# Reciprocal roots of the norms on GpSimd, and a longer page allowance, in a two-layer decoder step

## The chip, the cores and the metric

The kernel runs on one core of a Trainium2 chip. A core has five engines with instruction queues of their own: TensorE (PE, with PEld for its weight loads), VectorE (DVE), ScalarE (ACT), GpSimd (POOL) and SyncE (SP), and 16 DMA engines between the main memory and the on-chip memories. Each engine works through its queue in order, and waits on semaphores for what others make. The metric is the device time of one execution in microseconds (us), less is better; the median over runs counts.

## The reference

One inference step of two layers on 512 prompt tokens and 8 samples of 8 new tokens each (576 columns in all), float32, model width 1024. Layer 0 is a gated DeltaNet (a recurrence over chunks, 8 groups of two heads), layer 1 is differential attention over keys and values made by a shared projection, for the samples also over 1024 cached tokens each, in 8 pages of 128 tokens. What matters here are the norms:

```python
def rms_norm(x, gain):
    xf = x.astype(F32)
    y = xf * lax.rsqrt(jnp.mean(xf * xf, axis=-1, keepdims=True) + NORM_EPS)
    return (y * gain.astype(F32)).astype(x.dtype)

def l2_normalize(x):
    return x * lax.rsqrt(jnp.sum(x * x, axis=-1, keepdims=True) + NORM_EPS)
...
    q = jnp.repeat(l2_normalize(q.reshape(b, L, GDN_QK_HEADS, GDN_DK)) * GDN_DK ** -0.5, rep, axis=2)
    k = jnp.repeat(l2_normalize(k.reshape(b, L, GDN_QK_HEADS, GDN_DK)), rep, axis=2)
...
    o = rms_norm(o, out_gain) * jax.nn.silu(z.astype(F32)).reshape(b, L, GDN_V_HEADS, GDN_DV)
...
    k = partial_rotary(rms_norm(k.reshape(b, L, DIFF_HEADS, 2, DIFF_DH).astype(F32), k_gain), cos, sin)
...
    q = partial_rotary(rms_norm(q.reshape(b, L, DIFF_HEADS, 2, DIFF_DH).astype(F32), q_gain), cos, sin)
...
    o = rms_norm(o, sub_gain) * (1.0 - lam_init)
```

There is also a norm of the residual stream ahead of each layer and of the shared keys and values.

## The kernel before

Activations lie transposed, 128 of the model's dimensions on the partitions and the 576 tokens in two halves of 288 columns. A weight comes in sets of 1024 x 128 numbers (512 KB). For accuracy, weights and activations are each split into a rounded part and a rest (hi and lo); a product is three matrix products: hi by hi, hi by lo, lo by hi. In layer 0 the weights' rest is made by an accumulating DMA that POOL issues (L927, L937), in layer 1 by two POOL subtractions of 512 columns for each set (split_w, L2018).

The work runs in three stages: an opening (class Opening: the residual's norm and the first modulation), the first layer (class Weave) and the second (class Second). In each the order of the instructions on PE, ACT, DVE and POOL is laid out ahead of time by a planner in the kernel's own code: pieces of work are Python generators that yield an engine letter, a price in us and conditions, the planner keeps a clock for each engine, takes at each step the piece that can start first (a lower rank wins a tie), and fixes the resulting order of each engine. "E" and "L" stand for PE, "A" for ACT, "D" and "S" for DVE, "P" and "Q" for POOL. "S" and "P" also share a modelled port, so the plan lets no "S" step overlap a "P" step; "D" and "Q" do not take the port. A step behind another engine's starts HOP = 0.2 us after it, on PE PAD = 0.5 us. A room is one of a named set of buffers: a step that asks for one waits until it is left. A DMA is modelled as 2.3 us of latency, its price on a shared channel, and LATE = 0.6 us from its end until its data counts as landed.

The change touches these places:

- rsqrt (L160) and rsqrt_steps (L177): y = 1/sqrt(x) for a [128, n] tile, as an integer first guess (L167, L181), half of x (L169, L183) and three Newton steps of three instructions (L171 to L173, L186 to L188), 11 DVE instructions. rsqrt issues them as one step, rsqrt_steps as four, so that other DVE work can come between.
- Opening.sums: the root of the first norm, for 5 columns.
- Group.prep and Group.post: for each of the 8 groups of the first layer the keys' root (5 columns) and the output norm's (9 columns).
- second_norm: the residual's root in the second layer, once for each half.
- Tile2.rows: the 16 tiles of queries and keys, each evacuated by ACT, transposed, squared, summed over 64 (L2272), scaled (L2275), rooted (10 columns), multiplied by the root (L2278), and transposed back on PE. Tile2.rotary does the rotary part in four POOL instructions (L2304 to L2307) ahead of L2278.
- Prompt2.finish: the output norm of each of 8 attention heads over the prompt.
- samples_end: the output norm of the samples. The root is spread to all partitions by scaling the identity (L2638), a product with ones, and a copy to the on-chip memory (L2644).
- transfers (L333): what the planner takes as landed, and when. Cached pages ("kpage", "vpage") are loaded by Pages.loads into five rooms: POOL copies the page's number (L2471), SP reads it and issues the DMA (L2476). Sample2.keys (tile px) and Sample2.values (tile po) use two pages at a time on PE.

Of the other lines that the prediction names, L2224 evacuates a tile of the z projection of layer 1, and L1416 copies a part of the first layer's recurrence.

Of the kernel before, what the change touches and what calls it, by code (L numbers as in the profile page):

```python
# [10 lines left out]
F32 = mybir.dt.float32  # L11
F32R = mybir.dt.float32r
BF16 = mybir.dt.bfloat16
I32 = mybir.dt.int32
# [4 lines left out]
D = 1024  # L19
# [140 lines left out]
def rsqrt(K, pool, x, n, parts=128, tag="rs"):  # L160

    nc = K.nc
    y = pool.tile([128, n], F32, name=tag + "y", tag=tag + "y")
    t = pool.tile([128, n], F32, name=tag + "t", tag=tag + "t")
    xh = pool.tile([128, n], F32, name=tag + "h", tag=tag + "h")
    s = slice(0, parts)
    nc.vector.tensor_scalar(out=y[s].bitcast(I32), in0=x.bitcast(I32), scalar1=-0.5,  # L167
                            scalar2=float(0x5F3759DF), op0=ALU.mult, op1=ALU.add)
    nc.vector.tensor_scalar(out=xh[s], in0=x, scalar1=-0.5, scalar2=None, op0=ALU.mult)  # L169
    for _ in range(3):  # L170
        nc.vector.tensor_mul(out=t[s], in0=y[s], in1=y[s])  # L171
        nc.vector.tensor_mul(out=t[s], in0=t[s], in1=xh[s])
        nc.vector.scalar_tensor_tensor(out=y[s], in0=t[s], scalar=1.5, in1=y[s], op0=ALU.add, op1=ALU.mult)  # L173
    return y


def rsqrt_steps(K, pool, x, n, tag, us):  # L177

    nc = K.nc
    y, t, xh = (pool.tile([128, n], F32, name=tag + c, tag=tag + c) for c in "yth")  # L180
    nc.vector.tensor_scalar(out=y[:].bitcast(I32), in0=x.bitcast(I32), scalar1=-0.5,  # L181
                            scalar2=float(0x5F3759DF), op0=ALU.mult, op1=ALU.add)
    nc.vector.tensor_scalar(out=xh[:], in0=x, scalar1=-0.5, scalar2=None, op0=ALU.mult)  # L183
    for _ in range(3):
        yield "S", us
        nc.vector.tensor_mul(out=t[:], in0=y[:], in1=y[:])  # L186
        nc.vector.tensor_mul(out=t[:], in0=t[:], in1=xh[:])
        nc.vector.scalar_tensor_tensor(out=y[:], in0=t[:], scalar=1.5, in1=y[:], op0=ALU.add, op1=ALU.mult)  # L188
    return y
# [64 lines left out]
class Weave:  # L254
# [76 lines left out]
    def transfers(self, until):  # L331

        while True:  # L333
            act = [q for q in self.queues.values() if q]
            rate = SHARED if len(act) > 1 else 1.0
            lands = self.clock + min(q[0][0] for q in act) / rate if act else math.inf
            comes = self.coming[0][0] if self.coming else math.inf
            t = max(self.clock, min(lands, comes))
            if t > until or t == math.inf:
                return  # L340
            for q in act:
                q[0][0] -= (t - self.clock) * rate
            self.clock = t
            if comes <= lands:
                _, _, q, us, name = self.coming.pop(0)
                self.queues[q].append([us, name])
            else:
                for q in act:
                    if q[0][0] < 1e-9:
                        self.done[q.pop(0)[1]] = t + LATE, None  # L350
                return
# [95 lines left out]
class Opening(Weave):  # L447
# [95 lines left out]
    def sums(self):  # L543
# [16 lines left out]
        r = yield from rsqrt_steps(K, K.small, ms[:], nt, "rn", 0.6)  # L560
# [343 lines left out]
SB = 3  # L904
HELD = 4
# [132 lines left out]
class Group:  # L1038
# [196 lines left out]
    def prep(self):  # L1235
# [40 lines left out]
        yield "S", 0.6  # L1276
        ksum = A.sm.tile([128, 5], F32, name="ksum")
        nc.vector.tensor_scalar_add(out=ksum[:], in0=ssk[:], scalar1=4 * EPS)
        rk = yield from rsqrt_steps(K, A.sm, ksum[:], 5, "rs", 0.53)
# [205 lines left out]
    def post(self):  # L1485
# [4 lines left out]
        yield "S", 0.8, ("O", g), ("gdn", g), ("ssq", g), ("sq", g)  # L1490
# [5 lines left out]
        self.rs = yield from rsqrt_steps(K, A.sm, x[:], 9, "ro", 0.6)  # L1496
# [587 lines left out]
def second_norm(W, K, half):  # L2084
# [12 lines left out]
    yield "S", 0.3  # L2097
    r = yield from rsqrt_steps(K, P.ss, ms[:], 3, "rn", 0.6)
# [107 lines left out]
class Tile2:  # L2206
# [41 lines left out]
    def rows(self):  # L2248
# [25 lines left out]
        yield "S", 0.5  # L2274
        nc.vector.tensor_scalar(out=ss[:], in0=ss[:], scalar1=1.0 / 64, scalar2=EPS, op0=ALU.mult, op1=ALU.add)  # L2275
        r = yield from rsqrt_steps(K, P.tk, ss[:], 10, "rq", 0.6)
# [330 lines left out]
def samples_end(W, K):  # L2607
# [12 lines left out]
    yield "A", 0.65, Room("pg"), Room("pg")  # L2620
    r0, r1 = W.took
    ta, tb = (K.pg.tile([128, 8, 128], F32, name="pg")[:].rearrange("p a b -> p (a b)") for _ in range(2))
    sq, d, rt = ta[:, 0:512], ta[:, 512:1024], tb[:, 0:512]
# [10 lines left out]
    yield "S", 2.0  # L2634
    r = rsqrt(K, K.small, ms[:, 0:4], 4, tag="rn")
    yield "S", 1.15
    for c in range(4):
        nc.vector.tensor_scalar(out=d[:, 128 * c:128 * c + 128], in0=K.ident, scalar1=r[:, c:c + 1], scalar2=None, op0=ALU.mult)  # L2638
# [10 lines left out]
    W.leave(r0, r1)  # L2649
# [19 lines left out]
class Prompt2:  # L2669
# [81 lines left out]
    def finish(self, h):  # L2751
# [17 lines left out]
        W.leave(lr)  # L2769
        yield "D", 0.7  # L2770
# [272 lines left out]
def setup(K, ctx, ins):  # L3043
# [21 lines left out]
    K.asel = con[:, 128:e - s]  # L3065
    ones = K.per.tile([128, 128], F32, name="ones")
# [136 lines left out]
```

## Time and profile before

| | us |
|---|---|
| runs shown: median of 3 (lowest, highest) | 1199.89 (1198.29, 1205.4) |
| the profiled execution | 1203.46 |
| its span, from the first to the last instruction | 1201.7 |
| cached pages, 64 of keys and 64 of values, issue to landing (median) | 5.4 and 5.2 |
| bytes moved by DMA | 241.06 MB |

The profile gives each instruction's start and duration, its engine, line and tiles. A wait is idle time of an engine ahead of an instruction, put down to what ended last before it. Lines of the timeline read: start, duration, engine, line, operation, tile written and tiles read, shape, count where several are merged, and in brackets the idle time ahead of it with what ended it. Stages of the execution: the opening up to about 40 us, the first layer to about 660, the residual, q and k projections to 880, pages, prompt heads, v and z projections to about 1147, and the output projection.

### The profile page before, as it was taken

The numbers are of one execution on the slowest core, as the hardware profiler recorded it, in microseconds if no ns is written. First come the engines' busy times: TensorE is split into PE (matmuls) and PEld (weight loads), VectorE is DVE, ScalarE is ACT, GpSimd is POOL, SyncE is SP. The second block draws the span as 40 slices with busy tenths as digits, with TensorE's granted clock in tenths as the row PEclk, the third lists the DMA queues.
The fourth block names the chain that finished last, engine by engine and source line by source line (L and its number), as shares of the span: only waits on it lengthen the run. The fifth ranks groups of instructions, "written<-read, shape, count | busy, mean of one in ns | idle before, by whom it ended". The sixth has DMA issues, their size and how long they took to land.

```text
span 1201.7 us, 33311 instructions
## 1 busy us (share of the span) xinstructions
PE 1147.5 (95%) x12819; PEld 1050.2 (87%) x12819; DVE 766.7 (64%) x2223; ACT 688.0 (57%) x1894; POOL 373.8 (31%) x720
## 2 busy tenths in 40 slices
PE   8999999999999999899989999999999999998998
PEld 6899899998989998899988989998997777777998
DVE  5667876767877876668635467487644555555542
ACT  4766768677776867576545243865435545543430
POOL 2432322241322323232122340656524223121241
PEclk8999999999999999999999999999999999999999
DMA  9786667676666566566958985322948998993243
GB/s 363 211 216 161 156 158 165 178 168 185 175 175 174 135 173 153 179 176 172 255 164 232 337 283 181 106 66 79 346 154 310 326 334 304 346 329 100 58 125 116
DMA packets 87935, 241.06 MB, mean 201 GB/s; under 512 B 14482, under 2 KB 28690, under 8 KB 87778
## 3 DMA queue, kind: packets, MB, share of 16 engines
q1 hardware_dynamic: 71650, 180.22, 43.4%
q0 software_dynamic: 16128, 58.73, 22.2%
q8 instruction: 101, 1.65, 0.6%
q14 instruction: 56, 0.46, 0.1%
HBM read 213.07 MB, written 25.84 MB: 199 GB/s over the span
## 4 chain that ended last, share of the span: by engine, by line
PE 61%; DMA 14%; ACT 8%; issue 7%; DVE 6%; POOL 2%; SPq 1%; POOLq 0%; DVEq 0%; ACTq 0%
PE pp L292 16%; PE pp L1922 10%; PE pc L292 6%; DMA whi<-wall 5%; PE px L1922 5%; PE pq L1922 5%; PE pt L292 3%; PE sc L1922 3%; PE pt L1922 2%; DMA pg<-cv 2%; PE pt L1927 2%; PE po L1922 2%; PE pa L292 2%; PE pv L1922 2%; DMA pg<-ck 2%
## 5 line engine op out<-in xcount | busy, mean ns | idle before, releaser
L2018 POOL TENSOR_TENSOR wlo<-wraw,whi 128x512 fp32r<-128x512 f32 x94 | 122.8, 1327 | 179.0 <-ACT whi L2013 169.4
L292 PE MATMUL pp<-hlo,whi 128*128 128x288 f32 x592 | 172.3, 311 | 0.0
L292 PE MATMUL pp<-hhi,whi 128*128 128x288 f32 x592 | 163.1, 296 | 0.0
L1922 PE MATMUL pp<-hhi,whi 128*128 128x288 f32 x432 | 132.5, 307 | 3.0 <-DVE x L1821 2.3
L1922 PE MATMUL pp<-hlo,whi 128*128 128x288 f32 x432 | 127.6, 296 | 2.0 <-DVE hlo L1847 1.6
L1922 PE MATMUL pp<-hhi,wlo 128*128 128x288 f32 x432 | 125.9, 296 | 0.9 <-POOL wlo L2018 0.6
L292 PE MATMUL pp<-hhi,wraw 128*128 128x288 f32 x576 | 124.8, 301 | 0.0
L292 PEld LDWEIGHTS pp<-hlo,whi 128*128 128x128 f32 x592 | 112.3, 190 | 1.9 <-issue 1.2
L292 PEld LDWEIGHTS pp<-hhi,whi 128*128 128x128 f32 x592 | 112.5, 190 | 0.6
L292 PE MATMUL pp<-hhi,wlo 128*128 128x288 f32 x592 | 104.1, 303 | 0.1
L292 PEld LDWEIGHTS pp<-hhi,wraw 128*128 128x128 f32 x576 | 94.6, 190 | 0.5
L1922 PEld LDWEIGHTS pp<-hhi,whi 128*128 128x128 f32 x432 | 81.4, 188 | 6.6 <-issue 5.3
L1128 DVE SCALAR_TENSOR_TENSOR y<-u,vec,y 128x600 f32<-128x600 f32 x96 | 82.9, 865 | 5.6 <-ACT y L1125 5.1
L292 PEld LDWEIGHTS pp<-hhi,wlo 128*128 128x128 f32 x592 | 84.7, 188 | 2.0 <-issue 1.2
L292 PE MATMUL pp<-hlo,wraw 128*128 128x288 f32 x288 | 84.3, 315 | 0.0
L1922 PEld LDWEIGHTS pp<-hlo,whi 128*128 128x128 f32 x432 | 81.5, 189 | 2.7 <-DVE hlo L1847 2.1
L1922 PEld LDWEIGHTS pp<-hhi,wlo 128*128 128x128 f32 x432 | 80.7, 188 | 1.3 <-POOL wlo L2018 0.8
L937 POOL DMA_DIRECT2D wlo<-wall x38 | 33.7, 887 | 125.8 <-ACT wlo L932 84.9
L2471 POOL COPY pg<-ptt 1x1 int32<-1x1 int32 x128 | 25.8, 206 | 142.3 <-PE px L1922 78.4
L2013 ACT CAST whi<-wraw 128x1024 fp32r<-128x1024 f32 x47 | 49.0, 1046 | 33.8 <-DMA wraw<-wall 9.5
L1922 PE MATMUL pq<-hhi,whi 128*128 128x288 f32 x192 | 61.8, 322 | 3.1 <-DVE x L2224 2.9
L1922 PE MATMUL pq<-hhi,wlo 128*128 128x288 f32 x192 | 57.1, 297 | 0.0
(512 smaller groups left out, 3150.8 us busy)
## 6 DMA issues: line engine op xcount, KB each, us to landing
pg<-ck SPq DMA_DIRECT2D x64, 512.0 KB, 5.4
pg<-cv SPq DMA_DIRECT2D x64, 512.0 KB, 5.2
wraw<-wall SPq DMA_DIRECT2D x49, 512.0 KB, 4.4
whi<-wall POOLq DMA_DIRECT2D x38, 512.0 KB, 6.3
wlo<-wall POOLq DMA_DIRECT2D x38, 512.0 KB, 6.0
wraw<-wall POOLq DMA_DIRECT2D x36, 512.0 KB, 5.9
araw<-ada SPq DMA_DIRECT2D x24, 512.0 KB, 5.2
araw<-ada SPq DMA_DIRECT2D x8, 1024.0 KB, 14.6
```

Source lines behind the costliest of these rows:

```text
L292: return self.K.nc.tensor.matmul(**kw)
L937: K.nc.gpsimd.dma_start(out=lo[:], in_=src, accum_op=ALU.add)
L1128: nc.vector.scalar_tensor_tensor(out=y[:, :YW], in0=u[:, j:j + YW], scalar=cw[j], in1=y[:, :YW], op0=ALU.mult, op1=ALU.add)
L1922: return self.K.nc.tensor.matmul(**kw)
L1927: return self.K.nc.tensor.transpose(**kw)
L2013: nc.scalar.copy(out=hi[:], in_=raw[:])
L2018: nc.gpsimd.tensor_sub(out=lo[:, q:q + 4], in0=raw[:, q:q + 4], in1=hi[:, q:q + 4].bitcast(F32))
L2471: nc.gpsimd.tensor_copy(out=e, in_=P.ptt[0:1, i:i + 1])
```

## The change

The reciprocal root becomes one instruction on POOL, x to the power of -0.5, with a constant tile as the exponent, at all the places above: the 11 DVE instructions go, and the step is planned as "Q" at POW = 1.2 us. The planner counts a cached page as landed SPARE = 1.4 us after its modelled end instead of 0.6. At the samples' end the root is spread to all partitions by four products that read it as their broadcast weights, whose result the last multiplication reads where it lies, so the scalings of the identity, the copy and one of two page rooms go. In the prompt heads two small DVE instructions become one, and a room is left ahead of the root. Some prices of neighbouring "S" steps are lowered to what is left in them.

```diff
-def rsqrt(K, pool, x, n, parts=128, tag="rs"):
...
-    nc.vector.tensor_scalar(out=y[s].bitcast(I32), in0=x.bitcast(I32), scalar1=-0.5,
-                            scalar2=float(0x5F3759DF), op0=ALU.mult, op1=ALU.add)
-    nc.vector.tensor_scalar(out=xh[s], in0=x, scalar1=-0.5, scalar2=None, op0=ALU.mult)
-    for _ in range(3):
-        nc.vector.tensor_mul(out=t[s], in0=y[s], in1=y[s])
-        nc.vector.tensor_mul(out=t[s], in0=t[s], in1=xh[s])
-        nc.vector.scalar_tensor_tensor(out=y[s], in0=t[s], scalar=1.5, in1=y[s], op0=ALU.add, op1=ALU.mult)
-    return y
-
-
-def rsqrt_steps(K, pool, x, n, tag, us):
...
+def root(K, pool, x, n, tag):
+
     y = pool.tile([128, n], F32, name=tag + "y", tag=tag + "y")
...
+    K.nc.gpsimd.tensor_tensor(out=y[:], in0=x, in1=K.power.to_broadcast([128, n]), op=ALU.pow)
     return y
...
-                        self.done[q.pop(0)[1]] = t + LATE, None
+                        name = q.pop(0)[1]
+                        self.done[name] = t + (SPARE if "page" in str(name[0]) else LATE), None
...
+SPARE = 1.4
+POW = 1.2
...
# Opening.sums
-        r = yield from rsqrt_steps(K, K.small, ms[:], nt, "rn", 0.6)
+        yield "Q", POW
+        r = root(K, K.small, ms[:], nt, "rn")
...
# Group.prep
-        yield "S", 0.6
+        yield "S", 0.2
...
-        rk = yield from rsqrt_steps(K, A.sm, ksum[:], 5, "rs", 0.53)
+        yield "Q", POW
+        rk = root(K, A.sm, ksum[:], 5, "rs")
...
# Group.post
-        self.rs = yield from rsqrt_steps(K, A.sm, x[:], 9, "ro", 0.6)
+        yield "Q", POW
+        self.rs = root(K, A.sm, x[:], 9, "ro")
...
# Tile2.rows
-        yield "S", 0.5
+        yield "S", 0.2
         nc.vector.tensor_scalar(out=ss[:], in0=ss[:], scalar1=1.0 / 64, scalar2=EPS, op0=ALU.mult, op1=ALU.add)
-        r = yield from rsqrt_steps(K, P.tk, ss[:], 10, "rq", 0.6)
+        yield "Q", POW
+        r = root(K, P.tk, ss[:], 10, "rq")
...
# samples_end
-    yield "A", 0.65, Room("pg"), Room("pg")
...
+    yield "A", 0.65, Room("pg")
...
-    yield "S", 2.0
-    r = rsqrt(K, K.small, ms[:, 0:4], 4, tag="rn")
-    yield "S", 1.15
-    for c in range(4):
-        nc.vector.tensor_scalar(out=d[:, 128 * c:128 * c + 128], in0=K.ident, scalar1=r[:, c:c + 1], scalar2=None, op0=ALU.mult)
+    yield "Q", POW
+    r = root(K, K.small, ms[:, 0:4], 4, "rn")
...
-    K.mm(out=ps[:], lhsT=K.ones, rhs=d, start=True, stop=True)
-    yield "A", act(512)
-    nc.scalar.copy(out=rt, in_=ps[:])
-    W.leave(xr)
-    yield "S", 0.75
-    nc.vector.scalar_tensor_tensor(out=o, in0=rt.rearrange("p (h t) -> p h t", t=64), scalar=K.sg2[:, 0:1], in1=o,
+    for c in range(4):
+        K.mm(out=ps[:, 128 * c:128 * c + 128], lhsT=r[:, c:c + 1].to_broadcast([128, 128]), rhs=K.ident, start=(c == 0),
+             stop=(c == 3))
+    yield "D", 0.75
+    nc.vector.scalar_tensor_tensor(out=o, in0=ps[:].rearrange("p (h t) -> p h t", t=64), scalar=K.sg2[:, 0:1], in1=o,
                                    op0=ALU.mult, op1=ALU.mult)
...
# Prompt2.finish
-        yield "S", 2.7
+        yield "S", 0.4
...
-        nc.vector.tensor_mul(out=x[:], in0=ls[:, :, 0], in1=ls[:, :, 0])
-        nc.vector.tensor_scalar(out=x[:], in0=x[:], scalar1=EPS, scalar2=None, op0=ALU.mult)
+        nc.vector.scalar_tensor_tensor(out=x[:], in0=ls[:, :, 0], scalar=EPS, in1=ls[:, :, 0], op0=ALU.mult, op1=ALU.mult)
...
-        r = rsqrt(K, P.ss, x[:], 4, tag="ra")
         W.leave(lr)
+        yield "Q", POW
+        r = root(K, P.ss, x[:], 4, "ra")
...
# setup
+    power = K.per.tile([128, 1], F32, name="power")
+    nc.gpsimd.memset(power[:], -0.5)
+    K.power = power[:]
```

The output norm of Group.post and the first norm in second_norm are changed in the same way; the price of the "S" step ahead of the root falls from 0.8 to 0.4 in the first, and the step of 0.3 goes in the second.

More of the change, by code (lines that the diff above doesn't have):

```diff
@@ L157 @@
     pass
-def rsqrt(K, pool, x, n, parts=128, tag="rs"):
-    nc = K.nc
+def root(K, pool, x, n, tag):
     y = pool.tile([128, n], F32, name=tag + "y", tag=tag + "y")
[L164 to L167, printed above, removed]
-                            scalar2=float(0x5F3759DF), op0=ALU.mult, op1=ALU.add)
-    nc.vector.tensor_scalar(out=xh[s], in0=x, scalar1=-0.5, scalar2=None, op0=ALU.mult)
-    for _ in range(3):
-        nc.vector.tensor_mul(out=t[s], in0=y[s], in1=y[s])
-        nc.vector.tensor_mul(out=t[s], in0=t[s], in1=xh[s])
-        nc.vector.scalar_tensor_tensor(out=y[s], in0=t[s], scalar=1.5, in1=y[s], op0=ALU.add, op1=ALU.mult)
-    return y
-def rsqrt_steps(K, pool, x, n, tag, us):
[L179 to L188, printed above, removed]
+    K.nc.gpsimd.tensor_tensor(out=y[:], in0=x, in1=K.power.to_broadcast([128, n]), op=ALU.pow)
     return y
@@ L1489, in post @@
         last = g == G - 1
-        yield "S", 0.8, ("O", g), ("gdn", g), ("ssq", g), ("sq", g)
+        yield "S", 0.4, ("O", g), ("gdn", g), ("ssq", g), ("sq", g)
         x = A.sm.tile([128, 9], F32, name="ox")
@@ L2096, in second_norm @@
     nc.vector.tensor_scalar(out=ms[:], in0=ps[:, HT:HT + 3], scalar1=1.0 / D, scalar2=EPS, op0=ALU.mult, op1=ALU.add)
-    yield "S", 0.3
-    r = yield from rsqrt_steps(K, P.ss, ms[:], 3, "rn", 0.6)
+    yield "Q", POW
+    r = root(K, P.ss, ms[:], 3, "rn")
     yield "E", None
@@ L2619, in samples_end @@
     W.leave(xr)
-    yield "A", 0.65, Room("pg"), Room("pg")
-    r0, r1 = W.took
-    ta, tb = (K.pg.tile([128, 8, 128], F32, name="pg")[:].rearrange("p a b -> p (a b)") for _ in range(2))
-    sq, d, rt = ta[:, 0:512], ta[:, 512:1024], tb[:, 0:512]
+    yield "A", 0.65, Room("pg")
+    r0, = W.took
+    sq = K.pg.tile([128, 8, 128], F32, name="pg")[:].rearrange("p a b -> p (a b)")[:, 0:512]
     nc.scalar.activation(out=sq.rearrange("p (h t) -> p h t", t=64), in_=o, func=AF.Square)
@@ L2641, in samples_end @@
     ps = K.px.tile([128, 512], F32, name="px")
-    K.mm(out=ps[:], lhsT=K.ones, rhs=d, start=True, stop=True)
-    yield "A", act(512)
-    nc.scalar.copy(out=rt, in_=ps[:])
-    W.leave(xr)
-    yield "S", 0.75
-    nc.vector.scalar_tensor_tensor(out=o, in0=rt.rearrange("p (h t) -> p h t", t=64), scalar=K.sg2[:, 0:1], in1=o,
+    for c in range(4):
[3 more added lines that the diff above has]
+    nc.vector.scalar_tensor_tensor(out=o, in0=ps[:].rearrange("p (h t) -> p h t", t=64), scalar=K.sg2[:, 0:1], in1=o,
                                    op0=ALU.mult, op1=ALU.mult)
-    W.leave(r0, r1)
+    W.leave(xr, r0)
     yield from gated2(W, K, slice(0, 8), slice(SEQ, NT), 512, [("z", h, 1) for h in range(8)], ("gs",))
@@ L2762, in finish @@
         W.leave(pvr)
[L2763 removed]
+        yield "S", 0.4
         x = P.ss.tile([128, 4], F32, name="oxx")
[L2765 to L2766 removed]
+        nc.vector.scalar_tensor_tensor(out=x[:], in0=ls[:, :, 0], scalar=EPS, in1=ls[:, :, 0], op0=ALU.mult, op1=ALU.mult)
         nc.vector.scalar_tensor_tensor(out=x[:], in0=ms[:], scalar=1.0 / 128, in1=x[:], op0=ALU.mult, op1=ALU.add)
[L2768 removed]
         W.leave(lr)
+        yield "Q", POW
+        r = root(K, P.ss, x[:], 4, "ra")
         yield "D", 0.7
```

## Prediction

> **What bounds the kernel now.** I read the page first (busy shares), then the busy times by stage, then the waits of PE, and last the timeline around each wait of PE that a root stands behind.
>
> ```profile
> span 1201.7 us, 33311 instructions
> PE 1147.5 (95%) x12819; PEld 1050.2 (87%) x12819; DVE 766.7 (64%) x2223; ACT 688.0 (57%) x1894; POOL 373.8 (31%) x720
> ```
>
> PE is the bound: it is idle for 1201.7 - 1147.5 = 54.2 us. The change takes no matrix work away (below), so what it can win lies in these 54 us. By stage (columns: stretch, length, then busy time and count of PE, PEld, DVE, ACT, POOL, granted clock, DMA share, GB/s):
>
> ```profile
> 0.00:640.00 640.00, 615.52 (x6908) 569.89 (x6909) 448.48 (x1336) 429.12 (x1280) 185.27 (x388) 0.99 0.69 186
> 640.00:760.00 120.00, 114.45 (x1146) 109.44 (x1145) 73.65 (x182) 47.40 (x99) 38.17 (x37) 1.00 0.74 248
> 760.00:880.00 120.00, 113.01 (x1061) 109.62 (x1060) 86.43 (x259) 71.48 (x136) 68.89 (x116) 1.00 0.45 150
> 880.00:1100.00 220.00, 211.89 (x3042) 172.06 (x3041) 110.61 (x335) 111.50 (x319) 52.28 (x157) 1.00 0.84 295
> 1100.00:1202.00 102.00, 92.61 (x674) 89.16 (x672) 47.50 (x114) 28.49 (x61) 29.19 (x22) 0.97 0.31 94
> ```
>
> Idle of PE: 24.5 us in the first layer (0 to 640), 5.6, 7.0 in the stage of the q and k rows (760 to 880), 8.1 in the stage of the cache pages, 9.4 at the end. The waits of PE say for what (total us, times, longest):
>
> ```profile
> PE pc L292 <- ACT wv L1416: 4.7, 10, 1.3
> PE pt L1927 <- DVE qkt L2278: 4.5, 2, 2.7
> PE po L1922 <- DMA pg<-cv: 4.0, 7, 1.2
> PE pq L1922 <- DVE x L2224: 2.9, 3, 2.3
> PE pt L1927 <- DVE qss L2275: 1.8, 1, 1.8
> PE px L1922 <- DMA pg<-ck: 1.6, 3, 0.7
> PE pp L1922 <- POOL wlo L2018: 0.6, 1, 0.6
> ```
>
> The largest group is the first layer's chain on ACT; no root stands in it. The second, fourth and fifth are roots, as the timeline shows, and the third and sixth are the pages.
>
> **The change, part by part.** It has 44 places: 1 in the opening, 8 key norms and 8 output norms in the first layer, 2 residual norms, 16 q and k rows, 8 prompt heads and the samples' end in the second. Each drops 11 DVE instructions (484 in all) and gains one on POOL.
>
> *DVE freed.* The three lines of one Newton step, 48 times each in the 16 q and k rows:
>
> ```profile
> L187 DVE TENSOR_TENSOR rqt<-rqt,rqh 128x10 f32<-128x10 f32 x48 | 13.7, 285 | 1.7
> L188 DVE SCALAR_TENSOR_TENSOR rqy<-rqt,rqy 128x10 f32<-128x10 f32 x48 | 11.8, 246 | 1.6
> L186 DVE TENSOR_TENSOR rqt<-rqy 128x10 f32<-128x10 f32 x48 | 11.4, 239 | 0.7
> ```
>
> Undisturbed such an instruction takes 0.17 us (timeline below), in the rows 0.24 to 0.29 on average. The rows' nine steps are 13.7 + 11.8 + 11.4 = 36.9 us; 484 at 0.17 to 0.29 give 82 to 140, I take 100 us, out of 766.7. DVE is not the bound, so this counts only where PE waits on it.
>
> *Where PE waits for a root: the rows.* Why they are slower than 0.17 us:
>
> ```profile
> 808.89 0.22 DVE L2275 TENSOR_SCALAR qss<-qss 128x10 f32<-128x10 f32 x1
> 809.96 0.36 POOL L2307 TENSOR_TENSOR qkt<-rc,rsn 128x80 f32<-128x80 f32 x1
> 810.78 0.17 DVE L187 TENSOR_TENSOR rqt<-rqt,rqh 128x10 f32<-128x10 f32 x1
> 811.34 2.51 POOL L2018 TENSOR_TENSOR wlo<-wraw,whi 128x512 fp32r<-128x512 f32 x2 [1.02 <-ACT whi L2013]
> 811.40 1.25 DVE L187 TENSOR_TENSOR rqt<-rqt,rqh 128x10 f32<-128x10 f32 x1
> 812.69 1.19 DVE L188 SCALAR_TENSOR_TENSOR rqy<-rqt,rqy 128x10 f32<-128x10 f32 x1
> 813.98 1.03 DVE L2278 TENSOR_TENSOR qkt<-qkt,rqy 128x640 f32<-128x640 f32 x1
> 815.15 0.74 PE L1927 MATMUL pt<-con_ident,qkt 128*128 128x128 f32 x5 [2.71 <-DVE qkt L2278]
> ```
>
> The same DVE instruction takes 0.17 us alone and 1.25 when POOL's weight split begins just before it: it ends when POOL's first of two ends (811.34 + 1.26), the next when the second ends. Two such hits end in 2.71 us of idle PE. The other two waits in this stage:
>
> ```profile
> 775.19 0.74 PE L1927 MATMUL pt<-con_ident,qkt 128*128 128x128 f32 x5 [1.77 <-DVE qss L2275]
> 801.92 0.74 PE L1927 MATMUL pt<-con_ident,qkt 128*128 128x128 f32 x5 [1.74 <-DVE qkt L2278]
> ```
>
> Together 2.71 + 1.77 + 1.74 = 6.22 us. On POOL the root cannot collide with POOL's own split. In the first case its input is there at 809.11 and POOL has ended the rotary at 810.32; a power of 1.2 us ends at 811.5, and the multiplication starts then instead of at 813.98: 2.5 us sooner, 0.2 of the 2.71 stay. The multiplication itself still reads two tiles and can still be hit; I leave 0.8 us for that in the three, so -5.4.
>
> The Trainium skill (GPSIMD Engine Reference, 8. Key points) says that GpSimd shares its SBUF interfaces with VectorE, with contention for instructions that have two SBUF inputs; the rows above agree, 0.17 against 1.25 us. By that rule each power would also hold DVE off while it runs, which the rows of before cannot show.
>
> *The samples' end.*
>
> ```profile
> 1103.93 0.78 DVE L167 TENSOR_SCALAR rny<-nms 128x4 int32<-128x4 int32 x1
> 1106.32 0.16 DVE L173 SCALAR_TENSOR_TENSOR rny<-rnt,rny 128x4 f32<-128x4 f32 x1
> 1106.86 0.44 DVE L2224 SCALAR_TENSOR_TENSOR x<-scr,pq 128x288 f32<-128x288 f32 x1
> 1107.36 0.40 PE L1922 MATMUL pq<-hhi,whi 128*128 128x288 f32 x1 [2.26 <-DVE x L2224]
> ```
>
> The root holds DVE from 1103.93 to 1106.48 in one piece, the evacuation L2224 stands behind it, and PE waits 2.26 us for that bank. With the root on POOL this goes: -2.1 (0.2 kept for a later neighbour). The four scalings by the identity and the copy (L2638, L2644) go as well; one 512-column product becomes four of 128, the same columns with three more weight loads, which overlap other products. Nothing for either.
>
> *The other places.* Opening: the root's first and last instruction, the first product that reads it, and the stretch around it:
>
> ```profile
> 13.72 0.17 DVE L181 TENSOR_SCALAR rny<-nms 128x5 int32<-128x5 int32 x1
> 15.53 0.17 DVE L188 SCALAR_TENSOR_TENSOR rny<-rnt,rny 128x5 f32<-128x5 f32 x1
> 17.91 1.33 PE L292 MATMUL pa<-con_ident,rny 128*128 128x128 f32 x6
> 16.00:36.00 20.00, 18.91 (x196) 0.93 1.04 405
> ```
>
> An undisturbed root takes 15.70 - 13.72 = 1.98 us, and PE reads it 2.2 us after its end. DMA is full (share 1.04, the ada loads) from 16 to 36 us, so a sooner root is hidden; if that cover were gone, it would be worth at most 1.98 - 1.2 = 0.8 us. First layer, residual norms and prompt heads: none is named in a wait of PE, 0, with -4 to +3 kept for the range, since 17 x 2 us of DVE goes there.
>
> *The page allowance.* A page counts as landed 1.4 instead of 0.6 us after its modelled end, so its products are placed 0.8 us later in PE's fixed order. The waits for pages are 4.0 + 1.6 = 5.6 us in 10 pieces of at most 1.2; 0.8 later, little of each would be left. But a page read later frees its room later, the next load is issued later, and DMA is 0.84 busy there. I take half: -2.5; bounds -5 and +6 (below).
>
> *POOL's new work.* 44 powers. No row of before has one. Near rows:
>
> ```profile
> L2304 POOL TENSOR_TENSOR rc<-qkt,cosq x8: 519/533/979, 767.0 to 820.0; 128x160 f32<-128x160 f32 x8
> L2306 POOL TENSOR_TENSOR qkt<-rc,rsn x16: 351/354/389, 768.1 to 875.5; 128x80 f32<-128x80 f32 x16
> L2305 POOL TENSOR_TENSOR rsn<-qkt,sinq x8: 522/611/1106, 767.4 to 820.5; 128x160 f32<-128x160 f32 x8
> L2471 POOL COPY pg<-ptt x128: 173/174/1583, 672.8 to 1083.8; 1x1 int32<-1x1 int32 x128
> L2018 POOL TENSOR_TENSOR wlo<-wraw,whi 128x512 fp32r<-128x512 f32 x94 | 122.8, 1327 | 179.0 <-ACT whi L2013 169.4
> ```
>
> Least 0.17 us (one element); the longest row is 1.33, but a power is more work per element than a subtraction, so rows give no ceiling, and I keep 4 us as the far end, three times the longest row. I take 1.2, the plan's own price, because its other POOL prices agree with rows: 1.29 for the split (row 1.33), 1.85 for the four rotary instructions (0.53 + 0.61 + 0.35 + 0.36). 44 x 1.2 = 53 us lie beside PE: POOL is busy 31%, and 68.89 + 16 x 1.2 = 88 of 120 us in the fullest stage. What is queued behind them in order: weight splits, page copies and the first layer's weight loads. PE waited only 0.6 us for splits all told, so I add +1.5 for such delays.
>
> Sum: -5.4 - 2.1 - 2.5 + 1.5 = -8.5 us. The profiled execution took 1203.46 us (span 1201.7), 3.6 above the median of 1199.89; it becomes 1195.0, and the median 1191.4.
>
> **The rivals.**
> *Given back.* All instructions get new places from the planner, and waits that were hidden come forward. For it: only 13% of PE's idle time is the rows'. Then -1 to -2, 1198.5.
> *More than the waits.* The planner also reckons with about 100 us less DVE and may pack the 24.5 us of the first layer and the 5.6 after it better. If a third of these 30 goes, -10 on top: 1182.
> *The power is long (slower).* Place: the rows' stage, where POOL has 120 - 68.89 = 51 us free; 16 powers fill it at 3.2 us each. An undisturbed root on DVE takes 1.98 us, so from 2.0 us on each undisturbed row is later than now, and at 4 us POOL needs 68.9 + 64 = 133 us of 120, PE +13: 1199.9 + 13 = 1213. Holding DVE off for 16 x 4 us would add to it. Against it: the agreement of the other prices.
> *The allowance slows the pages.* Five rooms serve 128 pages; 0.8 us more per room and turn is 128/5 x 0.8 = 20 us on the pages' stretch if the rooms bind, of which products of the z projection cover most; PE would lose some 6: 1205. Against it: at DMA share 0.84 the transfers, not the rooms, set most of the pace.
>
> **How the numbers follow.** About 1% (12 us) is what a measurement of this kernel tells from no change. Forecast 1191.4 (own range 1186 to 1197): 0.42. Given back 0.22, more 0.20, long power 0.09, slow pages 0.07. Faster than 1187.9: 0.18 from "more" and 0.10 from the low part of the forecast, 0.28. Slower than 1211.9: 0.07 from the long power, 0.05 from slow pages and unlucky placement, 0.12. Within: 0.60. The range takes in most of "more" and "given back" and slow pages: 1180 to 1207.
>
> **What would show it.** Right: DVE near 665 us busy and 484 fewer instructions; POOL +44 instructions and about +53 us; no wait of PE on L2278 above 1 us between 760 and 820; no wait on L2224 above 1 us near the samples' end; waits for pages under 3 us in total. Wrong: a power over 2.0 us; POOL over 100 of 120 us in the rows' stage; PE's idle time still 54 us or more, under new names; or PE busy longer than 1147 us, which nothing here accounts for.

## The result, and the profile after

| | before | after |
|---|---|---|
| median, us (lowest, highest) | 1199.32 (1198.29, 1205.4) | 1185.38 (1184.48, 1191.14) |
| ratio, with its 95% interval | | 0.9866 [0.9834, 0.9899] |
| the profiled execution, us | 1203.46 | 1185.3 |
| its span, us | 1201.7 | 1183.3 |

By the two medians the kernel became 13.9 us faster; the ratio puts the gain at 1.3%. The two profiles differ by 18.4 us, because the one of before comes from an execution 4 us above its median; what follows from a pair of profiles is to be read with that in mind. The page of after, span and busy times:

```profile
span 1183.3 us, 32811 instructions
PE 1145.0 (97%) x12827; PEld 1048.3 (89%) x12827; DVE 685.8 (58%) x1727; ACT 689.8 (58%) x1893; POOL 453.5 (38%) x765
```

PE does the same work (1145.0 against 1147.5 us) and is idle for 38.3 instead of 54.2 us. DVE lost 496 instructions and 80.9 us (484 of the roots, the four scalings at the samples' end, one in each of 8 prompt heads), POOL gained 45 and 79.7 us. So almost the whole gain is idle time of PE that went.

Stages with fixed times would mix that with work that merely moved, so I cut both traces at the same events: the first weight product of the second layer (pp), the first sum of squares in the q and k rows (qss), the last pp product, the first output product (px). Busy time by stage of before, then of after (columns as in the prediction: stretch, length, PE, PEld, DVE, ACT, POOL, granted clock, DMA share, GB/s); the stages are first layer, residual norms with the first q and k products, rows, pages and all beside them, output:

```profile
0.00:655.40 655.40, 630.92 (x7026) 585.29 (x7027) 457.62 (x1364) 437.49 (x1303) 187.54 (x391) 0.99 0.69 186
655.40:765.80 110.40, 104.85 (x1072) 99.83 (x1071) 64.56 (x154) 44.77 (x85) 39.79 (x38) 1.00 0.72 250
765.80:900.20 134.40, 127.41 (x1310) 122.89 (x1309) 92.46 (x273) 72.42 (x140) 68.29 (x131) 1.00 0.45 152
900.20:1147.00 246.80, 235.72 (x3056) 194.01 (x3055) 133.73 (x392) 126.15 (x357) 63.88 (x150) 0.99 0.74 259
1147.00:1201.70 54.70, 48.58 (x365) 48.14 (x363) 18.30 (x43) 7.17 (x12) 14.30 (x12) 0.98 0.41 127
```

```profile
0.00:650.90 650.90, 630.92 (x7028) 583.33 (x7029) 430.19 (x1179) 440.60 (x1305) 218.96 (x409) 1.00 0.71 190
650.90:760.40 109.50, 106.41 (x1084) 102.44 (x1083) 61.31 (x131) 45.84 (x86) 41.47 (x39) 0.98 0.68 235
760.40:895.90 135.50, 128.58 (x1330) 121.95 (x1330) 60.73 (x97) 72.46 (x139) 104.19 (x150) 1.00 0.50 161
895.90:1129.90 234.00, 230.54 (x3029) 192.50 (x3028) 118.02 (x279) 125.01 (x358) 75.83 (x158) 1.00 0.79 269
1129.90:1183.30 53.40, 48.53 (x365) 48.06 (x363) 15.55 (x42) 5.87 (x8) 13.07 (x11) 0.99 0.41 124
```

Length less PE's busy time is PE's idle time:

| stage | length before, after | PE idle before, after |
|---|---|---|
| first layer | 655.4, 650.9 | 24.5, 20.0 |
| norms, first products | 110.4, 109.5 | 5.6, 3.1 |
| rows | 134.4, 135.5 | 7.0, 6.9 |
| pages | 246.8, 234.0 | 11.1, 3.5 |
| output | 54.7, 53.4 | 6.1, 4.9 |

Where the prediction had its largest term, in the rows, PE's idle time did not fall. What went is in the pages' stage and in the first layer. (Rows and pages are best added, as the cut between them passes through products that can go either side: 381.2 to 369.5 us.) The waits of PE in after that answer to those of before (total us, times, longest):

```profile
PE pt L1908 <- DVE qT L2271: 3.2, 3, 1.7
...
PE pt L1908 <- DVE qkt L2260: 2.7, 6, 1.2
PE pc L267 <- ACT wv L1396: 2.5, 7, 0.7
...
PE px L1903 <- DMA pg<-ck: 1.8, 2, 1.1
...
PE pq L1903 <- DVE x L2205: 1.0, 1, 1.0
...
PE po L1903 <- DMA pg<-cv: 0.3, 1, 0.3
```

(L2260 is before's L2278, L2205 its L2224, L1396 its L1416, L1999 its weight split L2018.) Pages: 5.6 us before, 2.1 now. Rows: three waits of 6.22 us, the longest 2.71, became nine of 3.2 + 2.7 = 5.9 us, the longest 1.75. The power itself, 40 of the 44 (duration in ns least/median/most, first and last start; the others have 3, 4 and 5 columns):

```profile
L163 POOL TENSOR_TENSOR rqy<-qss,power x16: 1953/1961/2099, 763.7 to 869.0; 128x10 f32<-128x10 f32 x16
L163 POOL TENSOR_TENSOR rsy<-ksum,power x8: 1196/1200/2032, 90.6 to 525.9; 128x5 f32<-128x5 f32 x8
L163 POOL TENSOR_TENSOR roy<-ox,power x8: 1822/1834/1975, 166.0 to 621.5; 128x9 f32<-128x9 f32 x8
L163 POOL TENSOR_TENSOR ray<-oxx,power x8: 996/1006/1008, 931.0 to 1094.3; 128x4 f32<-128x4 f32 x8
```

From 4 to 10 columns the time grows by 0.955 us, 0.16 for each column on 0.37 to 0.40 fixed. The plan's single 1.2 us is right at 5 columns; in the rows, with 10, a power takes 1.96. What that does there, in the timeline of after:

```profile
795.75 0.33 PE L1908 MATMUL pt<-con_ident,ch 128*128 128x128 f32 x1 [1.75 <-DVE qT L2271]
...
795.85 1.96 POOL L163 TENSOR_TENSOR rqy<-qss,power 128x10 f32<-128x10 f32 x1 [1.76 <-DVE qss L2256]
...
797.85 1.14 DVE L2260 TENSOR_TENSOR qkt<-qkt,rqy 128x640 f32<-128x640 f32 x1 [2.07 <-POOL rqy L163]
...
799.13 0.73 PE L1908 MATMUL pt<-con_ident,qkt 128*128 128x128 f32 x5 [0.65 <-DVE qkt L2260]
```

DVE stands idle for 2.07 us until the power ends, the multiplication is late, and PE's transposes wait for it. This is one form of the waits that replaced the collisions; the one of 1.75 us behind L2271 lies ahead of the power that is shown.

**What follows a long wait of PE.** The column of the granted clock has more in it than the averages above show. In before, around the wait of 2.28 us for L1717 in the first layer (up to 510.19 us) and the one of 2.26 us for L2224 at the samples' end (up to 1107.36 us), then in after behind its wait of 1.46 us (up to 460.51 us):

```profile
510.50:513.90 3.40, 3.40 (x17) 3.40 (x16) 2.27 (x9) 3.40 (x14) 1.19 (x5) 0.51 0.75 111
...
1107.80:1111.20 3.40, 3.40 (x13) 2.63 (x13) 1.20 (x5) 0.00 (x0) 0.00 (x0) 0.50 0.03 7
```

```profile
461.80:465.20 3.40, 3.40 (x17) 3.03 (x16) 3.26 (x11) 2.73 (x12) 1.79 (x6) 0.50 0.90 207
```

For 3.4 us the clock is half, and products that followed each other at 0.13 us follow at 0.24:

```profile
1104.68 0.29 PE L1922 MATMUL pq<-hlo,whi 128*128 128x288 f32 x1
1104.81 0.29 PE L1922 MATMUL pq<-hhi,wlo 128*128 128x288 f32 x1
...
1108.15 0.44 PE L1922 MATMUL pq<-hlo,whi 128*128 128x288 f32 x1
1108.39 0.44 PE L1922 MATMUL pq<-hhi,wlo 128*128 128x288 f32 x1
```

The traces of before, of after and of the 15 experiments below have 41 such stretches between 45 us and 30 us before the end, of 3.4 us or two or three times that (others lie in the opening and at the end). Every one begins in, or within 3.6 us after, a wait of PE of 1.3 us or more. Of the 88 waits of that length 42 were followed by one, of the 21 above 2.5 us 18, and of the 242 from 0.5 to 1.3 us none. So a long wait can cost more than its length; an estimate from the rows is 1.7 us, half of 3.4, for each stretch. Executions of one kernel differ with it: of the 63 executions of before that were made beside the experiments, the 14 with a mean granted clock of 0.995 or more took 1199.6 us in the median, the 19 with 0.991 or less 1205.2. After's four had 0.996 and 0.997, so the 14 us gained hold at a like clock too.

### The profile page after: what moved, and what is told of

Same layout as the page of the kernel before. It is cut to its first block, busy times and chain, and to the rows that moved or that the text cites. A ratio compares the mean times of both kernels' runs of the same rounds, so it can differ in the third digit from the quotient of the medians.

```text
span 1183.3 us, 32811 instructions
## 1 busy us (share of the span) xinstructions
PE 1145.0 (97%) x12827; PEld 1048.3 (89%) x12827; DVE 685.8 (58%) x1727; ACT 689.8 (58%) x1893; POOL 453.5 (38%) x765
## 4 chain that ended last, share of the span: by engine, by line
PE 69%; DMA 10%; ACT 7%; POOL 5%; DVE 5%; issue 4%; SPq 0%; POOLq 0%; DVEq 0%; ACTq 0%
PE pp L267 20%; PE pp L1903 8%; PE pc L267 7%; PE pq L1903 6%; PE px L1903 6%; PE sc L1903 3%; PE po L1903 3%; PE pt L1903 3%; DMA whi<-wall 3%; PE pa L267 3%; DMA araw<-ada 2%; PE pv L1903 2%; PE pt L1908 2%; PE pt L267 2%; DMA wraw<-wall 2%
## 5 line engine op out<-in xcount | busy, mean ns | idle before, releaser
L1999 POOL TENSOR_TENSOR wlo<-wraw,whi 128x512 fp32r<-128x512 f32 x94 | 126.1, 1361 | 99.2 <-ACT whi L1994 88.6
L2453 POOL COPY pg<-ptt 1x1 int32<-1x1 int32 x128 | 28.6, 230 | 153.7 <-PE px L1903 60.2
```

Source lines behind the costliest of these rows:

```text
L1999: nc.gpsimd.tensor_sub(out=lo[:, q:q + 4], in0=raw[:, q:q + 4], in1=hi[:, q:q + 4].bitcast(F32))
L2453: nc.gpsimd.tensor_copy(out=e, in_=P.ptt[0:1, i:i + 1])
```

## The experiments

The theory after the result: the allowance is worth more than predicted, the powers are worth about what was predicted in sum but not where it was predicted, since those of the rows are too long. Rivals: the powers did it all; the time is an accident of the new order, since any change of the plan's numbers gives another order. Each ratio below is to runs of the kernel before made beside it, whose medians lay between 1201.2 and 1205.4.

**The two parts apart.** First the allowance alone, on the kernel before:

```diff
-                        self.done[q.pop(0)[1]] = t + LATE, None
+                        name = q.pop(0)[1]
+                        self.done[name] = t + (SPARE if "page" in str(name[0]) else LATE), None
+SPARE = 1.4
```

> The kernel before with only the page allowance of 1.4 us; all roots stay on VectorE. Theory 'the allowance carries the attention stage' (PE's idle time from the first prompt products to the output projection fell from 11.1 to 3.5 us, the waits for pages from 5.6 to about 1): about -6 us against the kernel before, near 1193. Theory 'the roots carry it': -2.5 or less, 1197 or more. Theory 'placement' (any new order of the instructions moves the time by some us either way): no sign is forecast, anything within 6 us of before.

Then all the rest of the change without the allowance, called the powers alone, on the kernel after:

```diff
-SPARE = 1.4
+SPARE = 0.6
```

> The changed kernel with the page allowance back at 0.6 us. If the allowance is worth 6 us: about 1191, with PE's waits for pages back at 4 us or more. If the roots carry the gain: 1187 or less. With e1 it shows whether the two parts add up to the 14 us.

Measured: the allowance alone 1190.97 us, 0.9913 [0.9885, 0.9941], or -10.4 us; the powers alone 1197.58 us, 0.9959 [0.9931, 0.9986], or -4.9 us. The product of the two ratios, 0.9872, is that of the whole change within its interval. The waits of PE for pages, with the allowance alone and then with the powers alone:

```profile
PE po L1924 <- DMA pg<-cv: 1.4, 2, 1.1
...
PE px L1924 <- DMA pg<-ck: 1.0, 2, 0.6
```

```profile
PE px L1903 <- DMA pg<-ck: 4.7, 6, 1.1
PE po L1903 <- DMA pg<-cv: 4.4, 8, 1.0
...
PE px L1903 <- POOL pg L2453: 1.3, 2, 0.9
```

The allowance takes the pages' waits from 5.6 to 2.4 us. The powers alone raise them to 9.1, and rows and pages together take 380.8 us, before 381.2. A part of what the powers alone win is clock: all their ten executions have 0.995 or more, 0.997 in the median, the 27 of before beside them 0.993, and the nine of these with 0.995 or more took 1199.3 us, which leaves 1.8 us. So the powers did not do it all; the larger part is the allowance's.

**How long an allowance.** On the kernel after, SPARE = 1.0 and SPARE = 2.2:

```diff
-SPARE = 1.4
+SPARE = 1.0
```

> The changed kernel with a page allowance of 1.0 us, halfway between 0.6 (e2, 0.9959 of before) and 1.4 (0.9866): planned landing 4.85 us after issue against 5.2 and 5.3 in the traces. If the agreement counts: between the two, 0.990 to 0.993, with 2 to 5 us of waits for pages. If there is a threshold: at one of the two ends.

```diff
-SPARE = 1.4
+SPARE = 2.2
```

> The changed kernel with a page allowance of 2.2 us. With 1.4 the plan counts a page as landed 2.3 + 1.55 + 1.4 = 5.25 us after its issue, and the traces show 5.2 and 5.3; with 0.6 it was 4.45. If the gain is the agreement with the landing, 2.2 adds nothing: PE's waits for pages stay near 1 us, time within 3 us of the changed kernel (1183 to 1188). If more is simply better: below 1182. If five rooms bind, the page stretch grows by up to 20 us and some comes through: above 1189.

Measured: at 1.0, 1195.84 us, 0.9942 [0.9924, 0.9961]; at 2.2, 1188.67 us, 0.9886 [0.9855, 0.9917]. The waits for pages at 1.0, then at 2.2:

```profile
PE px L1903 <- DMA pg<-ck: 3.1, 6, 0.8
...
PE po L1903 <- DMA pg<-cv: 2.5, 5, 0.6
```

```profile
PE po L1903 <- DMA pg<-cv: 0.5, 1, 0.5
```

At 0.6, 1.0, 1.4 and 2.2 they are 9.1, 5.6, 2.1 and 0.5 us, and the ratios 0.9959, 0.9942, 0.9866 and 0.9886. The waits fall evenly, but the time is won between 1.0 and 1.4; at 1.0 a ratio of 0.990 to 0.993 had been expected. That is where the plan meets the chip. The DMA issues of after, with the median from issue to landing as the last number:

```profile
pg<-ck SPq DMA_DIRECT2D x64, 512.0 KB, 5.2
pg<-cv SPq DMA_DIRECT2D x64, 512.0 KB, 5.3
```

The plan reckons 2.3 us of latency, 1.55 for the transfer on an empty channel and the allowance: 4.45 us with 0.6, 4.85 with 1.0, 5.25 with 1.4. Beyond the measured 5.2 to 5.3 more allowance removes waits, but no time that can be told apart.

**Is it the order?** HOP raised by 5 ns changes no work, only the plan's ties, and so the order: first on the kernel after, then on the kernel before, then on the kernel before with the allowance of 1.4.

```diff
-HOP = 0.2
+HOP = 0.205
```

> The changed kernel with the planner's hop between engines at 0.205 instead of 0.2 us: no mechanism, only another order of some instructions. It shows what placement alone moves. If the 14 us hold as a mechanism: within 4 us of the changed kernel, 1181 to 1190; if they were a lucky order: 1192 or more.

> The kernel before with the planner's hop at 0.205 instead of 0.2 us and nothing else. It shows what placement alone moves: within 4 us of before, 1197 to 1205. If it falls by 8 or more, placement can give what the change gave.

> The kernel before with the hop at 0.205 us, as in e12 (1.0052 of before), and the page allowance of 1.4 us. If the allowance works by agreeing with the landing, the placement does not matter: about 0.9% below e12, 0.996 of before, and PE's waits for pages fall from about 4.5 us to under 2.5. If e1 was a lucky placement: within 0.3% of e12.

Measured: after in another order 1186.21 us, 0.9891 [0.986, 0.9923]; before in another order 1212.16 us, 1.0052 [1.0029, 1.0074]; the latter with the allowance 1203.13 us, 1.0 [0.9975, 1.0024]. An order alone is thus worth 0.5% in the one kernel, and in the other 0.25%, which the intervals don't tell from nothing. The 1212.16 us lie outside the 1197 to 1205 that had been expected. The first layer of before in the other order takes 665.3 us, 10 more with the same work, but 659.1 with the allowance, whose edit leaves that layer's order as it is: there no stretch at half clock is on record in the layer, in the run before it two. So 4 to 10 us belong to the order. In that order the allowance gains 0.5%, some 6 us, where it gained 10.4 in the first, and PE's idle time in the pages' stage falls by 4.8 us (10.9 to 6.1) against 5.2 (11.1 to 5.9). The pages' waits fall from 5.6 to 3.5 us, where under 2.5 had been expected. Near 5 us of idle time is what the mechanism gives in both; the rest of the 10.4 belongs to the order, or to the uncertainty of the ratios.

**The rows' and the first layer's powers.** From the kernel after, the rows' roots go back to DVE, then instead those of the first layer:

```diff
# Tile2.rows
-        yield "Q", POW
-        r = root(K, P.tk, ss[:], 10, "rq")
+        r = yield from rsqrt_steps(K, P.tk, ss[:], 10, "rq", 0.6)
```

> The changed kernel with the 16 q and k rows' roots back on VectorE as Newton steps, the other 28 on GpSimd. The prediction's step (waits of PE behind the rows' roots, -5.4 us) says about +5: 1190. The rival, read from the two traces (PE idle in the rows' stage 7.0 before, 6.9 after, GpSimd busy 104 of 136 us there with powers of 1.96 us each): the rows gave nothing, within 1.5 us of the changed kernel, 1184 to 1187, or faster.

```diff
# Group.prep
-        yield "Q", POW
-        rk = root(K, A.sm, ksum[:], 5, "rs")
+        rk = yield from rsqrt_steps(K, A.sm, ksum[:], 5, "rs", 0.53)
# Group.post
-        yield "Q", POW
-        self.rs = root(K, A.sm, x[:], 9, "ro")
+        self.rs = yield from rsqrt_steps(K, A.sm, x[:], 9, "ro", 0.6)
```

> The changed kernel with the first layer's 16 roots (keys and output norms) back on VectorE. The prediction costed these at nothing: within 1 us of the changed kernel, 1185. The traces say the first layer ends 4.5 us sooner after the change with the same busy time of PE: if the roots there do that, +4.5, 1190.

(The price of the "S" step ahead goes back as well, in each.) Measured: rows on DVE 1193.56 us, 0.9935 [0.9911, 0.9959]; first layer on DVE 1191.22 us, 0.9914 [0.9878, 0.995]. The rows' waits come back as collisions (one of 2.7 us for the multiplication), PE's idle time in the rows is 8.5 us against 6.9 with the powers. That is 1.6 us, but the ratios differ by 0.7%, 8 us, and their intervals don't overlap: the prediction's step said +5, and the rival that the rows gave nothing falls. Most of the rest is the clock. The profile is of the fastest of the ten executions (1187.61 us, granted clock 0.996); the other one with 0.995 took 1188.72 us, the eight with 0.989 to 0.993 took 1192.55 to 1197.29. The traces say where: rows with all their Newton steps have a wait of 2.7 us behind a collision in all five traces that have such rows, and in four of the five, not in before's, half clock follows it. In after the longest wait of the rows is 1.75 us, and none follows. With the first layer on DVE that layer takes 653.1 us, with the powers 650.9; the 1191.22 us lie near the 1190 of the second expectation, but the ratios' intervals overlap.

**How long is the power, and does its length matter?** On the kernel after, in the same order of all instructions, a product stands in place of the power:

```diff
-    K.nc.gpsimd.tensor_tensor(out=y[:], in0=x, in1=K.power.to_broadcast([128, n]), op=ALU.pow)
+    K.nc.gpsimd.tensor_tensor(out=y[:], in0=x, in1=K.power.to_broadcast([128, n]), op=ALU.mult)
-    nc.gpsimd.memset(power[:], -0.5)
+    nc.gpsimd.memset(power[:], 1e-6)
```

> The changed kernel with the same order of instructions, but each power replaced by a product with 0.000001, so the roots themselves are left out and the norms' values are not the reference's. A product of 10 columns should take about 0.2 to 0.3 us instead of 1.96. It bounds what the powers' length costs: if they lie beside PE everywhere, within 1 us of the changed kernel; if the rows' stage pays for them, PE's 5.9 us of waits there fall to under 2 and the time by 3 to 5 us.

Measured: 1178.49 us, 0.9815 [0.979, 0.9839]. The instruction in the rows, and their stage:

```profile
L163 POOL TENSOR_TENSOR rqy<-qss,power x16: 201/207/428, 762.6 to 861.8; 128x10 f32<-128x10 f32 x16
```

```profile
759.30:888.70 129.40, 127.22 (x1331) 122.09 (x1330) 57.23 (x97) 72.20 (x140) 72.36 (x150) 1.00 0.51 169
```

With 0.21 in place of 1.96 us PE is idle there for 2.2 instead of 6.9 us. So the idle time that the prediction promised to end in the rows was there to be had, and the length of the power took it: 4.7 us.

The counterpart, on the kernel before: one Newton step of three, with every other instruction in before's order.

```diff
 # rsqrt
-    for _ in range(3):
+    for _ in range(1):
 # rsqrt_steps
-        yield "S", us
+        if (yield "S", us) or _: continue
```

> The kernel before in the same order on PE, ACT and GpSimd, with one Newton step in each root instead of three: two of the three steps are left out, so the roots are less exact, and VectorE runs 264 instructions fewer. If VectorE's time on the steps makes the waits that the prediction named: the two rows' waits on L2278 and the one of 2.3 us on L2224 go under 1 us each, PE's idle time in the rows' stage falls from 7.0 to under 3, and the time by 6 to 9 us, near 1193. For the first layer: if VectorE's time there is what the powers free, its idle time of 24.5 us falls to about 20 with this too; if it is the new order of the plan, it stays at 24.

Measured: 1194.83 us, 0.9912 [0.9883, 0.9942]. First layer and rows:

```profile
0.00:654.30 654.30, 628.50 (x7026) 583.95 (x7027) 439.73 (x1262) 436.27 (x1303) 187.56 (x391) 0.99 0.69 187
...
764.90:893.60 128.70, 127.07 (x1310) 122.95 (x1309) 70.45 (x177) 72.22 (x141) 68.33 (x132) 1.00 0.47 159
```

In the rows PE's idle time falls from 7.0 to 1.6 us and one wait of 0.87 is left of the three: a short root does end those waits. At the samples' end, in the same order, the wait of 2.26 us for L2224 falls with the shorter root:

```profile
1099.73 0.40 PE L1922 MATMUL pq<-hhi,whi 128*128 128x288 f32 x1 [1.02 <-DVE x L2224]
```

In the first layer, 102 DVE instructions less change nothing (idle 25.8 us, before 24.5). What was won in that layer does not come from DVE's time in a given order.

**The price put right.** On the kernel after, at all seven places, with the number of columns for n:

```diff
-        yield "Q", POW
+        yield "Q", 0.38 + 0.16 * n
```

> The changed kernel with each power planned at what the trace shows, 0.38 + 0.16 us for each column (1.98 for 10 columns instead of 1.2). If the waits of PE behind L2260 and L2271 in the rows' stage (5.9 us) come from the plan's too low price, they go to under 3 us and the time falls by 2 to 4 us: near 1182. If GpSimd's load there (104 of 136 us) makes them: the same waits, within 1.5 us of the changed kernel.

Measured: 1181.83 us, 0.9839 [0.9817, 0.9862], a little faster than after, though the intervals overlap. The time is the one expected, but not for the reason: PE is idle in the rows for 5.6 us, 4.3 of them still behind L2260, so the price did not make those waits. What became shorter is the first layer, 643.6 us, in another order. Three experiments start from this version. Two take the rotary's products, or all four of its instructions, back to DVE, since POOL had become the fullest engine beside PE in the rows:

```diff
-        yield "Q", 1.85, ("tabs",)
+        yield "S", 0.7, ("tabs",)
-        nc.gpsimd.tensor_mul(out=rc[:], in0=t[:, :, 0:16], in1=cos)
-        nc.gpsimd.tensor_mul(out=rsn[:], in0=t[:, :, 0:16], in1=sin)
+        nc.vector.tensor_mul(out=rc[:], in0=t[:, :, 0:16], in1=cos)
+        nc.vector.tensor_mul(out=rsn[:], in0=t[:, :, 0:16], in1=sin)
+        yield "Q", 0.75
```

> The kernel with priced powers (1181.8 us), and the rotary's two products of 160 columns moved from GpSimd to VectorE in the 16 rows: about 18 us less on GpSimd, 10 us more on VectorE in the rows' stage. If GpSimd's load there is what is left of the cost (PE idle 5.6 us, waits behind L2260 4.3): 1.5 to 3 us faster, near 1179.5. If not: within 1.5 us of 1181.8.

The second has the step as "S" at 1.2 us and all four instructions on nc.vector.

> As the run before, with all four rotary instructions on VectorE: GpSimd 102 down to about 72 us in the rows' stage. If GpSimd's load decides: PE's idle time in that stage under 4 us and 3 to 4 us faster than 1181.8, near 1178. The rival: the four read two tiles each, so the weight splits on GpSimd hold them up as they held the Newton steps, and the wait moves to L2260 again: 1182 or more.

The third gives two other loads of the plan a longer allowance:

```diff
-                        self.done[name] = t + (SPARE if "page" in str(name[0]) else LATE), None
+                        self.done[name] = t + {"kpage": SPARE, "vpage": SPARE, "xin": 2.0, "raw": 1.2}.get(name[0], LATE), None
```

> The kernel with priced powers (e6, 0.9839 of before) and two more loads of the second layer counted as landed later: the residual's pieces by 2.0 instead of 0.6 us after their modelled end (issue to landing 3.4 us planned, 3.7 to 5.9 in the traces), the weights by 1.2 (4.4 planned, 4.4 to 5.1). If the rule carries over, PE's waits behind the residual's loads (L1802, 1.3 us in e6) go, and 1 to 3 us with them: 0.982. If those loads have time to spare, within 0.2% of e6.

Measured: products on DVE 1193.62 us, 0.9912 [0.9883, 0.9941], worse than 0.9839, which neither expectation had (its granted clock is 0.990 in the median, with 20 us at half clock in the profile up to 920 us behind waits of 1.9 to 3.7 us: long waits again); all four on DVE 1184.33 us, 0.9826 [0.9796, 0.9855]; other landings 1181.53 us, 0.9832 [0.9797, 0.9867]. The last two are no better than the priced version; the wait behind L1802 that the landings should have ended stays, at 1.4 us. The waits of the rows with the products on DVE, and then with all four there:

```profile
PE pt L1908 <- DVE qkt L2260: 3.5, 1, 3.5
...
PE pt L1908 <- DVE qT L2271: 2.3, 2, 1.9
```

```profile
PE pt L1908 <- DVE qT L2271: 4.5, 1, 4.5
```

POOL's time in the rows' stage falls from 102 to 84 and 73 us, but a single wait of 3.5 or 4.5 us opens: the instructions are ones of DVE, as in before. A freer POOL by itself wins nothing there.

## Why the prediction was right or wrong

The time, 1185.4 us, lay in the range of 1180 to 1207, but the prediction was wrong in what it held likeliest, a change within 1% (0.60): the kernel became faster by 1.3%, for which 0.28 had been given, by 13.9 us instead of the 8.5 of the sum. Three steps failed: half of the pages' term was taken off, the power in the rows was taken at 1.2 us where it takes 1.96, and every wait was counted at its idle time alone, with nothing for the half clock behind a long one. The sum's terms:

- **The rows, -5.4: the step failed, though the powers there are worth as much.** The three waits were put down rightly (a short root ends them, 7.0 to 1.6 us of idle time), but the step "a power of 1.2 us ends at 811.5" took the plan's price for the chip's. At 1.96 us the nine waits add up to 5.9, against 6.22. The prediction supported the price by POOL's other prices, which agree with rows; that says nothing of an operation no row has. Its own point from which the rows lose was 2.0 us, so the power came out just on the harmless side of it. Taking these powers away costs 8 us all the same, but not by the way that was forecast, so a size near the -5.4 would be luck: 1.6 us of it is idle time, most of the rest the half clock behind the long waits, which the sum did not have, although its table showed a granted clock of 0.99 and 0.97 in two stages. The pair of profiles hides this, as in before's the wait of 2.71 us was not followed by half clock. The two signs named for this step failed as well: a wait of 1.16 us on L2260 at 812 us (the 1.2 in the list of waits), and POOL over 100 of 120 us in the stretch of time that was named:

```profile
760.00:880.00 120.00, 113.08 (x1127) 107.76 (x1126) 57.86 (x89) 67.98 (x131) 102.45 (x138) 1.00 0.46 148
```

- **The samples' end, -2.1: right in mechanism, but not alone.** With one Newton step in before's order the wait of 2.26 falls to 1.02 us, so the root's length did make it. No wait of PE stands there in after (its 1.05 us for L2205 comes at 1127 us, and stands with the allowance alone and with the powers alone too). But with the allowance alone, where the root is still on DVE, the 2.26 us are gone also, with 0.55 and 0.67 us in their place. So another order is enough to end it. In before half clock followed it, some 1.7 us more that the term did not count.
- **The pages, -2.5: the mechanism was right, the size wrong.** It is -5 to -10 us. The prediction set "half" against a feared later reload of the rooms, for which no run shows a sign: DMA's share in that stage rose from 0.74 to 0.79 and its rate from 259 to 269 GB/s. The rows that decide it were in the front table: 5.4 and 5.2 us from issue to landing, against the 4.45 of the plan. A plan that is 0.75 to 0.95 us early at every page, with 10 waits of at most 1.2, is mended by 0.8, and almost nothing should have been taken off the 5.6 us.
- **The first layer, 0: it became shorter, by the order.** The layer takes 650.9, 652.6, 648.2, 653.9 and 652.5 us in five runs with powers priced at 1.2 there and HOP at 0.2, and 655.4, 654.5, 654.3 and 653.1 in the four with Newton steps: 2.7 us on the mean, 4.5 in the pair of profiles. The five have one order of this layer among them, so the 5.7 us between them are not the edits': the run of 648.2 has no stretch at half clock in the layer, the others one or two (or one twice as long). It is not DVE's time in a fixed order (one Newton step: no gain). In before's order PE has waits there of 2.28 and 2.09 us, both for ACT, and half clock behind each; in after the longest is 1.46. The profile names no root for them, so what is left is the new order that the plan finds with DVE less filled; another order alone moves this layer by 4 to 10 us. Whether any plan with powers is better there than one without, a handful of orders can't settle.
- **POOL's new work, +1.5: not seen.** PE's wait for a weight split, 0.6 us before, is gone in after. POOL got 79.7 us instead of 53, some 68 of them in powers by the medians above. DVE lost 80.9, not 100, 0.163 for each of 496 instructions and just under the low bound: most of them had run undisturbed.

In sum, PE's idle time behind the terms of -5.4, -2.1, -2.5, 0 and +1.5 came out at about 0, -2 (shared with the allowance), -5 to -10, -3 to -5 and 0, and the stretches at half clock that went with the long waits come on top. The figures of single runs can't be added to 14, as each belongs to an order of its own. That the total was missed by only 6 us is luck in part: the rows, too high in idle time, hide some of what the pages and the first layer lacked. Of the rivals "more than the waits" came nearest with 1182: PE's idle time in its two stretches fell by 7.0 us in the pair of profiles, where it reckoned with a third of 30. "The allowance slows the pages" fell, and "the power is long" missed its point by 0.04 us. "Given back" is seen only without the new allowance, where the pages' waits rise from 5.6 to 9.1.

The Trainium skill (SBUF — State Buffer, Who interferes with whom) says that a DVE instruction with two SBUF inputs contends with a GpSimd instruction that reads SBUF, through a lock on the shared ports that is exclusive. The prediction feared by such a rule that each power would hold DVE off. Here the trace differs: DVE's products of two tiles while a power runs, in the first layer of after, with one before and one behind it:

```profile
165.84 0.22 DVE L1569 TENSOR_TENSOR tp<-XT,LA 128x64 f32<-128x64 f32 x1
166.01 1.83 POOL L163 TENSOR_TENSOR roy<-ox,power 128x9 f32<-128x9 f32 x1 [5.45 <-DVE ox L1474]
...
166.34 0.26 DVE L1569 TENSOR_TENSOR tp<-XT,LA 128x96 f32<-128x96 f32 x1
...
167.37 0.29 DVE L1569 TENSOR_TENSOR tp<-XT,LA 128x128 f32<-128x128 f32 x1
...
168.01 0.33 DVE L1569 TENSOR_TENSOR tp<-XT,LA 128x160 f32<-128x160 f32 x1
```

They grow evenly with their columns, 0.22, 0.26, 0.29, 0.33, and the two in the middle began and ended inside the power's 1.83 us.

## What to carry to other kernels

Where an order is laid out by a planner, hold each of its constants against the median of the trace, the landing of a DMA above all: one constant that was 0.8 us short cost this kernel more than 44 roots on the wrong engine did (10.4 and 4.9 us, each part alone). Count a wait of the bounding engine with what follows it: here a few long waits cost more than many short ones of the same sum, as only waits from 1.3 us on were followed by half clock. A profile is one execution; where a few such stretches decide, compare its time with the others'. An operation that no row has is to be priced by a measurement at its own width, and moving work to a freer engine shortens nothing where the chain that is waited for gets no shorter. Before a gain of half a per cent is credited to an edit of a planned kernel, measure what another order of the same work does, here up to 0.5%.

## What the runs showed of the hardware

A power on GpSimd takes 1.00, 1.20, 1.83 and 1.96 us for 4, 5, 9 and 10 columns on 128 partitions, 0.38 + 0.16 us for each column, where a product of 10 columns in its place takes 0.21 and a subtraction of 512 columns 1.33. So nearly all of the 0.16 us a column comes with the power, not with the columns. And it doesn't hold DVE off as the 512-column subtraction does (0.17 to 1.25 us in the prediction's timeline): of 47 DVE instructions with two tensors as inputs that overlap a power in after, and no weight split, none took over 1.04 times the median of the same instruction without one. Why was not tested.

PE's clock falls to half for 3.4 us or a multiple of it behind waits of PE: 41 of 41 stretches in the middle of the 17 traces begin in or up to 3.6 us after a wait of 1.3 us or more, 18 of 21 waits above 2.5 us were followed by one, and none of the 242 from 0.5 to 1.3 us.
